# Adding a finished pair of rows to the residual with an accumulating DMA

## The chip, the cores and the metric

The kernel runs on one core of a Trainium2 chip. The metric is device microseconds of one execution; the median of three runs of the kernel before is 1159.39 us (1158.99 to 1159.63).

A core has engines that run beside each other, each with its own queue of instructions in a fixed order: TensorE (PE in the profile, matrix products; PEld are its weight loads), VectorE (DVE, element-wise work), ScalarE (ACT, element-wise functions and copies), GpSimd (POOL, element-wise work, and it issues transfers) and SyncE (SP, which here only issues transfers). Transfers (DMAs) are carried out by DMA engines. An instruction that needs another engine's result waits on a semaphore, and everything behind it in the same queue waits with it.

## The reference

Two transformer layers over 512 tokens of width 1024, in float32: a hybrid attention layer, a neighbourhood attention layer, and after each a squared-ReLU MLP whose result is added to the residual h. Cut to what matters:

```python
def sq_relu_mlp(h, w_up, w_down):
    u = jax.nn.relu(h @ w_up)
    return (u * u) @ w_down

for layer in range(DEPTH):                  # DEPTH = 2, D_MODEL = 1024, D_FF = 4096
    hn = rmsnorm(h, norm_mix[layer])
    h = h + attention(layer, hn)
    h = h + sq_relu_mlp(rmsnorm(h, norm_ffn[layer]), ffn_w_up[layer], ffn_w_down[layer])
return rmsnorm(h, final_norm)
```

## The kernel before

The residual lies transposed in SBUF as `hT`, 128 partitions x 8 blocks x 512 tokens; a block is 128 of the 1024 features. Every float32 operand of a product is split into a high and a low part, and a product is three matmuls (high x high, high x low, low x high).

The second product of each MLP (`u * u` times `w_down`) is cut in parts over the 4096 inner features (`mlp`, from line 1476):

- first an ordinary product over 6 inner blocks, written into `hT` by `ev` (L1505), one block at a time;
- then `product8`, over 10 inner blocks, also added by `ev`;
- then the seven-block product: `u7.run(ids[m], evac)` in the loop `for m in range(4)` (L1539 to L1546). It multiplies 2x2 blocks with seven products in place of eight. Each m makes two blocks (a pair of rows of blocks) of the result, over 14 inner blocks in layer 0 (7 chunks of weights) and 12 in layer 1 (6 chunks);
- last, an ordinary product over the remaining 2 (layer 0) or 4 (layer 1) inner blocks. In layer 0 it adds to `hT` with `ev` again (L1505). In layer 1 `last_mlp` does it with the tokens on the partitions: `turn` (L1919) transposes `hT` on TensorE, the first four blocks while the products of m = 2 and m = 3 run (`beside`, L1976), the last four in `down` after m = 3 (L1950).

A chunk of weights of the seven-block product (`seven_chunk`, L319) goes through four engines. SyncE issues its load of 256 KB (L324) into a slot of the shared pool (`Slot`, names `a` in the profile) if one is to be had, else into one of four `raw` buffers. GpSimd makes the four sums from it in three instructions (L326 to L328). ScalarE makes the high parts, `whi` (L332), VectorE the low parts, `wlo` (L333). TensorE uses the chunk in 21 matmuls (L418 to L420). A chunk is asked for five chunks ahead of its use (`LOAD`) and split two ahead (`AHEAD`). A later ordinary chunk is loaded at L211 or L214 and split at L233 and L223.

When the chunks of an m are done, `Seven.run` (L406) puts the pair together from the four PSUM banks in a slot `w_` of its own: one copy of ScalarE (L426) and four adds of VectorE (L427 to L430). Then `evac` (L1541) adds `w_` to the two blocks of `hT` (L1543), and the slot is given back (L432). Slots are given out first in, first out, so the slot of a finished pair soon takes a later chunk's weights, a later pair or a part of the next layer's input.

Nobody writes out the order of the instructions here: the framework's scheduler places each engine's instructions by its own estimate of when they can run, but for those marked to be kept in program order. After layer 0 the next layer's input is split by ScalarE and VectorE (L579, L580), its squares are summed (L587, L589), and TensorE reduces them (L594).

The chunks used in the loop over m are, in order of use, 7 for each m in layer 0 and 6 in layer 1. In layer 0 the slot of the first pair takes the last chunk of m = 1, that of the second pair the first chunk of m = 3; in layer 1 the slot of the first pair takes the first chunk of m = 2.

Of the kernel before, what the change touches and what calls it, by code (L numbers as in the profile page):

```python
# [12 lines left out]
ALU = mybir.AluOpType  # L13
# [22 lines left out]
def encoder_kernel(ctx: ExitStack, tc: tile.TileContext, ins, out, dbg=None):  # L36
    nc = tc.nc
    PE, ACT, DVE, POOL, SP = nc.tensor, nc.scalar, nc.vector, nc.gpsimd, nc.sync
# [299 lines left out]
    class Seven:  # L338
# [29 lines left out]
        def split(self, kp, held=lambda z: z):  # L368

            for b in range(7):  # L370
                i = self.number(kp, b) // 2
                if i not in self.slots:
                    self.slots[i] = Slot()
            raw, t = self.raw.pop(kp)
            own = isinstance(t, Slot)
            r, t_ = (s_.rearrange("p (b n) -> p b n", n=256) for s_ in (raw.t, t.t if own else t))

            T4 = t_[:, 2:3] if own else r[:, 3:4]
            src = lambda b, n: (r[:, 1 + b : 1 + b + n] if b < 3 else t_[:, b - 3 : b - 3 + n] if b < 5
                                else r[:, 0:1] if b == 5 else T4)  # L380
            b = 0
            while b < 7:
                q = self.number(kp, b)
                n = 2 if b == 3 or (b < 2 and q % 2 == 0) or (b == 5 and not own) else 1
                d = self.slots[q // 2].t.rearrange("p (q z n) -> p q z n", q=2, z=2)[:, q % 2 : q % 2 + n]
                s_ = r[:, 0:4:3] if b == 5 and n == 2 else src(b, n)
                ACT.activation(d[:, :, 0], s_, AF.Copy)
                held(DVE.tensor_tensor(d[:, :, 1], s_, f32(d[:, :, 0]), op=ALU.subtract))
                b += n
                yield  # L390
                if b == 3 and not own:
                    held(DVE.tensor_tensor(r[:, 3], r[:, 3], r[:, 0], op=ALU.subtract))
                    yield
            raw.free()
            if own:
                t.free()
# [94 lines left out]
    def product8(w, first, U, evac, eng=None):  # L491


        nk = len(U)
        ids = [plan([(0, D, rows(w, k, 1))], 1, D, None, eng) for k in first]

        def run():
            banks = group(4) + group(4)

            def one(k, j):  # L500

                wh, wl = (z[:, 0, P * j : P * j + P] for z in weights(ids[k], AHEAD - (k == 1 or k == nk - 1 and j < 7)))
                x = U[k].pair()
                mm3(banks[j], wh, wl, x[:, 0, :], x[:, 1, :], k == 0, k == nk - 1)


            for js in (range(4), range(4, 8)):
                for k in (0, 1):
                    for j in js:
                        one(k, j)  # L510
                        yield MM3
            U[0].free()
            U[1].free()
            for k in range(2, nk - 2):
                for j in range(8):
                    one(k, j)
                    yield MM3
                U[k].free()
            for j in range(8):
                for k in (nk - 2, nk - 1):  # L520
                    one(k, j)
                    yield MM3

                if j < 5:
                    evac(j, banks[j])
            for j in range(5, 8):
                tc.keep_in_program_order(evac(j, banks[j]))
            U[nk - 2].free()
            U[nk - 1].free()

        return run()
# [4 lines left out]
    def tiles(c0, n):  # L536
        return [(c0 + o, min(P, n - o)) for o in range(0, n, P)]
# [903 lines left out]
    def bias_rows():  # L1441
        R, Fi, Fe = Slot(F32), Slot(F32), Slot(F32)
        rpb = ins["od_rpb"][0]
        for qr in range(8):
            SP.dma_start(R.t[16 * qr : 16 * qr + 16, 0:248],
                           rpb.rearrange("h a b -> h (a b)")[:, (7 - qr) * 31 : (7 - qr) * 31 + 248])
            yield
        POOL.memset(Fi.t[:, 0:376], NEG)
        POOL.memset(Fe.t[:, 256:512], NEG)
        rv = R.t[:, 0:248].rearrange("p (k d) -> p d k", d=31)  # L1450
        POOL.tensor_copy(Fi.t[:, 0:376].rearrange("p (j k) -> p j k", k=8)[:, 15:31, :], rv[:, 7:23, :])
        POOL.tensor_copy(Fe.t[:, 0:248].rearrange("p (j k) -> p j k", k=8), rv)
        for _ in range(6):
            yield
        bxv = bx.rearrange("h t (c r) k -> t c r h k", r=8)
        for c in range(16):
            SP.dma_start(bxv[0, c].rearrange("r h k -> r h k"), Fi.t[:, (15 - c) * 8 : (15 - c) * 8 + 256])
            yield

            v, off = (1, (7 - c) * 8) if c < 8 else (0, (23 - c) * 8)  # L1460
            SP.dma_start(bxv[1, c][:, :, 128 * v : 128 * v + 128], Fe.t[:, off : off + 128])
            yield
            SP.dma_start(bxv[1, c][:, :, 128 - 128 * v : 256 - 128 * v], Fe.t[:, 256:384])
            yield
        for s_ in (R, Fi, Fe):
            s_.free()
        yield

    def convert(u7, R):
        held = tc.keep_in_program_order  # L1470
        for kp, raw in enumerate(R):
            yield from u7.sums(kp, raw, DVE, held)
            yield
            yield from u7.split(kp, held)

    def mlp(l, last=None):

        stage, ahead, later = first_product(l)
        reserve[0] = 3
        w = ins["ffn_w_down"][l]
        up4, gens4 = [], []

        def plain_last(k0, V):
            left = list(V)
            gens4.extend(product(w, k0, up4, tiles(512 * c, 512), lambda j, b, c=c: ev(4 * c + j, b), nk=2 * len(V))
                         for c in range(2))

            def beside(m, i):
                if m == 0 and i % 8 == 4 and left:
                    w_ = left.pop(0)
                    for z in range(2):
                        U4.append(Slot())
                        up4.append(U4[-1].pair())
                        split(w_.t[:, S * z : S * z + S], up4[-1])
                    w_.free()

            return beside  # L1500

        U4 = []

        def ev(m, b):
            return DVE.tensor_tensor(hT[:, m, :], hT[:, m, :], b, op=ALU.add)  # L1505

        U, _, _, (at_u, _), _ = stage(SIZES[l][0])
        up = [s_.pair() for s_ in U]
        gens = [product(w, at_u, up, tiles(512 * c, 512), lambda j, b, c=c: ev(4 * c + j, b)) for c in range(2)]
        ahead()  # L1510
        for c, gen in enumerate(gens):
            for i, _ in enumerate(gen):
                later(c, i)
        for s_ in U:
            s_.free()
        U, R, V, (at_u, at_r), late = stage(*SIZES[l][1:])
        first = [k + z for k in at_u for z in range(2)]
        gen = product8(w, first, U, ev)
        u7 = Seven(2 * len(R))
        ids = [u7.plan(w, 256 * m, at_r) for m in range(4)]  # L1520
        k0 = 32 - 2 * len(V)
        beside = (last or plain_last)(k0, V)
        bias = iter(()) if last else bias_rows()
        reserve[0] = NSLOT
        work, at = convert(u7, R), 0
        for i, _ in enumerate(gen):
            if i in (1, 4, 6):
                next(late, None)
            next(bias, None)

            at += 9 * len(R) + 2
            while at > 0:
                next(work, None)
                at -= 8 * len(U) - 2
        for x in (work, bias):
            for _ in x:
                pass
        reserve[0] = 1
        for m in range(4):  # L1539

            def evac(w_):  # L1541
                h2 = hT[:, 2 * m : 2 * m + 2, :]
                DVE.tensor_tensor(h2, h2, w_.t.rearrange("p (z n) -> p z n", z=2), op=ALU.add)  # L1543

            for i, _ in enumerate(u7.run(ids[m], evac)):
                beside(m, i)  # L1546
        u7.free()
        for gen in gens4:
            for _ in gen:
                pass  # L1550
        for s_ in U4:
            s_.free()
# [487 lines left out]
```

## Time and profile before

| What | us |
|---|---|
| median of the runs | 1159.39 |
| profiled execution, span from its first to its last instruction | 1157.2 |
| median of the runs less this span (start and end) | 2.2 |
| busy: TensorE | 1146.8 |
| busy: VectorE | 903.0 |
| busy: ScalarE | 652.1 |
| busy: GpSimd | 577.5 |

The profile is of one execution, which has no time of its own but its span; the runs that were timed lie within 0.64 us of each other. A row of the timeline gives the start in us, the duration in us, the engine, the line of the kernel, the operation, and out<-in with shapes; a number in square brackets is how long the engine sat idle before, and what ended that. Rows of grouped instructions give count, shortest, median and longest time in ns. A matmul is pipelined, so its start tells more than its end. SPq and POOLq are the queues of SyncE and GpSimd.

### The profile page before, as it was taken

What the parts mean: (1) busy time and instruction counts of PE and PEld (TensorE: products, weight loads), DVE (VectorE), ACT (ScalarE), POOL (GpSimd) and SP (SyncE); (2) the same over time, 40 slices, a digit from 0 to 9 for tenths busy, and PEclk for the clock granted to TensorE, in tenths of its full rate; (3) what the DMA queues carried; (4) which work ended last, traced back from release to release, by engine and by line L of the source; (5) the groups of instructions that cost most, each with busy time, mean ns of one, the idle gap of its engine ahead of it and who ended that gap; (6) DMA issues with size and microseconds to landing.
All of it is one profiled execution on the core that took longest, in us unless ns stands there. A gap on an engine that the chain in (4) does not pass through costs nothing.

```text
span 1157.2 us, 20288 instructions
## 1 busy us (share of the span) xinstructions
PE 1146.8 (99%) x7276; PEld 1021.1 (88%) x7276; DVE 903.0 (78%) x1542; ACT 652.1 (56%) x1115; POOL 577.5 (50%) x708
## 2 busy tenths in 40 slices
PE   9999999999999999999999999999999999999997
PEld 7787888888899999899988998988889999988996
DVE  7887988878978887877685666668987788778675
ACT  6676876755346667433454556555553666743345
POOL 4366252216798882379402232231379889316930
PEclk9999999999999999999999999999999999999999
DMA  8322415122432326523436664443333233432332
GB/s 241 100 74 70 101 51 142 55 67 98 126 93 74 92 83 202 185 92 117 125 98 164 150 174 128 117 109 117 100 120 108 79 89 92 136 102 80 98 106 73
DMA packets 112148, 128.05 MB, mean 111 GB/s; under 512 B 9411, under 2 KB 94576, under 8 KB 112048
## 3 DMA queue, kind: packets, MB, share of 16 engines
q1 hardware_dynamic: 109424, 120.09, 35.4%
q0 software_dynamic: 2304, 6.31, 2.3%
q8 instruction: 57, 0.93, 0.4%
q14 instruction: 43, 0.35, 0.1%
q10 hardware_dynamic: 320, 0.36, 0.1%
HBM read 104.32 MB, written 6.29 MB: 96 GB/s over the span
## 4 chain that ended last, share of the span: by engine, by line
PE 96%; DVE 2%; DMA 1%; issue 1%; ACT 0%; POOL 0%; DVEq 0%; POOLq 0%
PE mm L573 9%; PE mm L575 9%; PE mm L574 9%; PE mm L418 4%; PE mm L420 4%; PE mm L419 4%; PE s L1097 3%; PE t L418 3%; PE t L420 3%; PE t L419 3%; PE o L1085 3%; PE s L573 3%; PE s L574 3%; PE s L575 3%; PE s L418 2%; PE s L420 2%
## 5 line engine op out<-in xcount | busy, mean ns | idle before, releaser
L573 PE MATMUL mm<-a,whi 128*128 128x512 f32 x440 | 178.6, 407 | 0.2
L332 ACT ACTIVATE whi<-a 128x896 fp32r<-128x896 f32 x105 | 99.7, 951 | 132.5 <-POOL a L328 39.2
L574 PE MATMUL mm<-a,whi 128*128 128x512 f32 x440 | 173.5, 394 | 0.0
L575 PE MATMUL mm<-a,wlo 128*128 128x512 f32 x440 | 173.5, 395 | 0.0
L333 DVE TENSOR_TENSOR wlo<-a,whi 128x896 fp32r<-128x896 f32 x105 | 133.1, 1272 | 49.2 <-ACT whi L332 46.1
L223 DVE TENSOR_TENSOR wlo<-raw,whi 128x1024 fp32r<-128x1024 f32 (+4 forms) x113 | 131.1, 1164 | 39.0 <-ACT whi L233 38.4
L233 ACT ACTIVATE whi<-raw 128x1024 fp32r<-128x1024 f32 (+3 forms) x116 | 109.1, 942 | 68.4 <-PE s L574 24.0
L418 PE MATMUL mm<-a,whi 128*128 128x256 f32 x410 | 115.1, 281 | 0.0
L420 PE MATMUL mm<-a,wlo 128*128 128x256 f32 x410 | 114.7, 280 | 0.0
L419 PE MATMUL mm<-a,whi 128*128 128x256 f32 x410 | 114.7, 280 | 0.0
L328 POOL TENSOR_TENSOR a<-a 128x128 f32<-128x128 f32 x105 | 102.9, 980 | 8.2
L326 POOL TENSOR_TENSOR a<-a 128x128 f32<-128x128 f32 x105 | 75.8, 722 | 57.3 <-DMA a<-in_ffn_w_up_dram 37.1
L575 PEld LDWEIGHTS mm<-a,wlo 128*128 128x128 f32 x440 | 82.5, 188 | 18.9
L573 PEld LDWEIGHTS mm<-a,whi 128*128 128x128 f32 x440 | 82.7, 188 | 17.6 <-issue 0.6
L574 PEld LDWEIGHTS mm<-a,whi 128*128 128x128 f32 x440 | 82.9, 188 | 15.3 <-DVE a L930 0.2
L327 POOL TENSOR_TENSOR a<-a 128x256 f32<-128x256 f32 x105 | 90.6, 863 | 8.2
L333 DVE TENSOR_TENSOR wlo<-raw,whi 128x896 fp32r<-128x896 f32 x51 | 62.4, 1226 | 35.4 <-ACT whi L332 35.4
L1683 POOL TENSOR_SCALAR p<-p,ti 128x256 f32<-128x256 f32 x64 | 35.6, 567 | 104.7 <-DVE ti L1682 91.5
L1105 POOL TENSOR_SCALAR p<-p,ti 128x512 f32<-128x512 f32 x64 | 45.0, 705 | 85.7 <-DVE ti L1104 63.6
L418 PE MATMUL t<-a,whi 128*128 128x256 f32 x296 | 83.1, 281 | 0.0
L419 PE MATMUL t<-a,whi 128*128 128x256 f32 x296 | 82.8, 280 | 0.0
L420 PE MATMUL t<-a,wlo 128*128 128x256 f32 x296 | 82.8, 280 | 0.0
(427 smaller groups left out, 3492.9 us busy)
## 6 DMA issues: line engine op xcount, KB each, us to landing
a<-in_ffn_w_up_dram SPq DMA_DIRECT2D x78, 256.0 KB
raw<-in_ffn_w_down_dram SPq DMA_DIRECT2D x38, 512.0 KB
raw<-in_od_w_qkv_dram SPq DMA_DIRECT2D x64, 128.0 KB
a<-in_ffn_w_down_dram SPq DMA_DIRECT2D x27, 256.0 KB
raw<-in_ffn_w_up_dram SPq DMA_DIRECT2D x26, 256.0 KB
raw<-in_ffn_w_down_dram SPq DMA_DIRECT2D x25, 256.0 KB
raw<-in_ffn_w_up_dram SPq DMA_DIRECT2D x12, 512.0 KB
a<-a SPq DMA_DIRECT2D x18, 256.0 KB
```

The costliest lines, as they stand in the source:

```text
L223: z = lambda: (eng or DVE).tensor_tensor(to, src, f32(high), op=ALU.subtract)
L233: ACT.activation(hi[:, 0:m], raw[:, 0:m], AF.Copy)
L327: POOL.tensor_tensor(r[:, 4:6], r[:, 2:3].to_broadcast([P, 2, P]), r[:, 0:7:6], op=ALU.add)
L328: POOL.tensor_tensor(r[:, 7], r[:, 3], r[:, 5], op=ALU.subtract)
L332: ACT.activation(hi[:, 0:896], raw[:, 128:1024], AF.Copy)
L333: DVE.tensor_tensor(lo[:, 0:896], raw[:, 128:1024], f32(hi[:, 0:896]), op=ALU.subtract)
L418: PE.matmul(o, wh, x[:, 0], start=kp == 0 and n in (0, 1, 3, 5), stop=False, skip_group_check=True)
L419: PE.matmul(o, wh, x[:, 1], start=False, stop=False, skip_group_check=True)
L420: PE.matmul(o, wl, x[:, 0], start=False, stop=kp == self.np - 1, skip_group_check=True)
L573: PE.matmul(o, wh, xh, start=first, stop=False)
L574: PE.matmul(o, wh, xl, start=False, stop=False)
L575: PE.matmul(o, wl, xh, start=False, stop=last)
```

## The change

The add of L1543 is no longer an instruction of VectorE. GpSimd's queue issues a DMA that reads the pair `w_` (128 x 1024 float32, 512 KB) and adds it to the two blocks of `hT` in place. It is done eight times, four in each layer.

```diff
             def evac(w_):
                 h2 = hT[:, 2 * m : 2 * m + 2, :]
-                DVE.tensor_tensor(h2, h2, w_.t.rearrange("p (z n) -> p z n", z=2), op=ALU.add)
+                POOL.dma_start(h2, w_.t.rearrange("p (z n) -> p z n", z=2), accum_op=ALU.add)
```

What the scheduler makes of it, by the order of instructions in both programs: VectorE's queue loses eight instructions, GpSimd's gains eight issues. In layer 0 the DMA of m = 0 stands behind the sums of four chunks that are loaded into `raw` and `a` buffers and ahead of the sums of the chunk that takes slot 6190; that of m = 1 stands behind the sums of raw 6471; those of m = 2 and m = 3 stand behind all sums of the layer. In layer 1 the DMA of m = 0 stands behind the sums of the chunks in slots 12365 and 12406, that of m = 1 behind those of slot 12597, the other two behind all sums. The loads into the slots of the first pairs (6160, 6411 and 12436) now wait for the DMA in SyncE's queue, and each is put one place later among the loads and the sums. The transposes of L1919 that read a pair wait for its DMA; the first of them in layer 1 is put in two halves around three matmuls. In the next layer's input of layer 0, the split of one block (its slot is that of m = 3's pair) waits for that pair's DMA, and the reduction of the squares on TensorE (L594) stands some five matmuls earlier.

## The prediction

> **What bounds the kernel now.** I read the page's engine line, then the chain of waits, then line L1543 by itself.
>
> ```profile
> span 1157.2 us, 20288 instructions
> PE 1146.8 (99%) x7276; PEld 1021.1 (88%) x7276; DVE 903.0 (78%) x1542; ACT 652.1 (56%) x1115; POOL 577.5 (50%) x708
> PE 96%; DVE 2%; DMA 1%; issue 1%; ACT 0%; POOL 0%; DVEq 0%; POOLq 0%
> L1543 DVE TENSOR_TENSOR hT<-hT,a x8: 1218/1389/1556, 526.3 to 1128.9; 128x1024 f32<-128x1024 f32 x8
>   PEld mm L1919: 0.2, 1
> ```
>
> TensorE is busy for 1146.8 of 1157.2 us, so whatever VectorE is relieved of can hardly be gained; what counts is whether TensorE is made to wait. The eight adds cost VectorE some 8 x 1.39 = 11.1 us, and only one instruction ever waited for one, 0.2 us. Then I looked at the stretch that follows layer 0's first add, at ScalarE's waits around layer 1's first add, and at the chain where VectorE is on it.
>
> ```profile
> 522.50:540.00 17.50, 17.50 (x151) 17.50 (x150) 12.85 (x14) 6.94 (x9) 16.47 (x20) 1.00 0.34 106
> 586.72 1.40 DVE a L580 x3
> ACT whi L332 <- POOL a L328: 11.7, 5, 3.3
> ```
>
> The columns of the first row are time, TensorE, weight loads, VectorE, ScalarE, GpSimd, each with its instructions, then clock, DMA share and GB/s. GpSimd, 50% busy over the span, is 94% busy (16.47/17.50) here: it makes the sums of the next weight chunks, and ScalarE waits for them (third row, from 1079 to 1101 us, 11.7 us in five waits). The new DMA is put into this queue.
>
> **The change part by part.** Removed: eight VectorE adds, 11.1 us, beside TensorE work. The one place where VectorE sets the end is 586 to 598 us (second row above: there the chain of waits runs through it), and layer 0's last add, one of the short ones (1.22 us), lies ahead of it; at most 1.2 us is to be had there.
>
> Added: eight issues on GpSimd and eight landings that replace the end of the add. Their price:
>
> ```profile
> L1591 POOL DMA_DIRECT2D a<-a x16: 512/525/640, 610.6 to 755.0; - x16
> DMA to landing us min/median/max: 2.8/3.7/4.0
> a<-a POOLq DMA_DIRECT2D x16, 256.0 KB, 3.7
> a<-in_ev_a_q_norm_dram POOLq DMA_DIRECT2D x2, 0.2 KB, 3.3
> q0 software_dynamic: 2304, 6.31, 2.3%
> ```
>
> An issue holds GpSimd for 0.53 us; 8 x 0.53 = 4.2 us. No accumulating DMA and none of 512 KB from this queue is in the trace, so the landing L is bounded. Below: 3.3 us for 0.2 KB and 3.7 for 256 KB give 4.1 for 512 KB, if adding costs nothing. Above: the queue's 6.31 MB took 2.3% of the span, 26.6 us of all 16 engines, so 512 KB take 2.2 us; fetching the destination as well makes it 4.4, and 3.3 + 4.4 = 7.7. I take the middle, L = 6.0. The Trainium skill, "DMA: Bandwidth & Descriptors", section "Anatomy of one DMA — SWDGE (gpsimd) path", fits 2.0 us + bytes/436e3, an estimate of 3.2 us here; the 3.7 us for half the bytes says it is too short for this kernel, and by it the sum below would be about 6 us instead of 20.
>
> Three things now wait for a landing: the load that takes over the buffer of the finished pair (in SyncE's queue, with all loads behind it), the transposes of hT on TensorE, and the layer's last pair.
>
> *Layer 0, first pair.*
>
> ```profile
> 525.59 0.69 DVE L430 TENSOR_TENSOR a<-a,o 128x512 f32<-128x512 f32 x1
> 526.32 1.56 DVE L1543 TENSOR_TENSOR hT<-hT,a 128x1024 f32<-128x1024 f32 x1
> 526.87 1.33 POOL L328 TENSOR_TENSOR raw<-raw 128x128 f32<-128x128 f32 x1
> 527.90 0.37 SPq L324 DMA_DIRECT2D a<-in_ffn_w_down_dram  x1
> 532.35 0.46 POOL L326 TENSOR_TENSOR a<-a 128x128 f32<-128x128 f32 x1
> 534.12 0.46 POOL L326 TENSOR_TENSOR a<-a 128x128 f32<-128x128 f32 x1
> 535.19 2.43 DVE L333 TENSOR_TENSOR wlo<-a,whi 128x896 fp32r<-128x896 f32 x2 [3.11 <-ACT whi L332]
> 537.59 0.28 PE L420 MATMUL mm<-a,wlo 128*128 128x256 f32 x1
> ```
>
> Before, the add ends at 527.88 and the load into its buffer is issued at 527.90. That chunk's low parts are ready at 536.4 and used at 537.59: 1.2 us of slack. In the changed program's order the DMA stands behind the sums that end at 528.2, so it lands at 528.2 + 6 = 534.2 and frees the load only then. A load's own price:
>
> ```profile
> 1101.37 1.64 SPq L324 DMA_DIRECT2D a<-in_ffn_w_down_dram  x2
> 1104.09 0.47 POOL L326 TENSOR_TENSOR a<-a 128x128 f32<-128x128 f32 x1 [0.34 <-DMA a<-in_ffn_w_down_dram]
> 1087.44 0.95 ACT L332 ACTIVATE whi<-a 128x896 fp32r<-128x896 f32 x1 [2.40 <-POOL a L328]
> ```
>
> Load 2.8 us (1101.37 to 1104.09, and its issue), sums 1.9 at their fastest (532.35 to the next chunk's at 534.12, VectorE idle), high part 1.0, low part 1.2: 534.3 + 6.9 = 541.2. TensorE loses 541.2 - 537.6 = **3.6 us**.
>
> *Layer 0, second pair.* GpSimd's sums ahead of this DMA run on from 539.0 for the 11.9 us that the same four chunks took before (536.63 to 548.52), less some contention: issue at 550, landing 556, load, sums and splits to 563.
>
> ```profile
> 536.63 1.31 POOL L326 TENSOR_TENSOR raw<-raw 128x128 f32<-128x128 f32 x1
> 548.06 0.46 POOL L328 TENSOR_TENSOR raw<-raw 128x128 f32<-128x128 f32 x1
> 554.78 1.17 DVE L333 TENSOR_TENSOR wlo<-a,whi 128x896 fp32r<-128x896 f32 x1 [2.70 <-PE o L419]
> 557.41 0.28 PE L420 MATMUL mm<-a,wlo 128*128 128x256 f32 x1
> ```
>
> TensorE, already 3.6 late, wants it at 557.41 + 3.6 = 561.0: **2.0 us**.
>
> *Layer 0, last pair.* Nothing is ahead of this DMA. Landing at 578.7 + 6 = 584.7, while the next layer's third split (its buffer is the pair's) would run at about 583.
>
> ```profile
> 577.99 0.68 DVE L430 TENSOR_TENSOR a<-a,s 128x512 f32<-128x512 f32 x1
> 586.63 3.40 DVE L580 SCALAR_TENSOR_TENSOR a<-hT,gT,a 128x512 fp32r<-128x512 f32 x5
> ```
>
> The splits and adds behind it in VectorE's queue end at 590.6 instead of 590.03: **0.6 us**, the relief of 1.2 us already in it. Bounds -1.2 to 3.
>
> *Layer 1, first pair.*
>
> ```profile
> 1081.45 0.69 DVE L430 TENSOR_TENSOR a<-a,o 128x512 f32<-128x512 f32 x1
> 1086.94 0.46 POOL L328 TENSOR_TENSOR a<-a 128x128 f32<-128x128 f32 x1
> 1092.71 2.44 DVE L333 TENSOR_TENSOR wlo<-a,whi 128x896 fp32r<-128x896 f32 x2 [3.12 <-ACT whi L332]
> 1093.93 0.38 PE L420 MATMUL s<-a,wlo 128*128 128x256 f32 x1
> ```
>
> The pair is finished at 1082.1, but the DMA's place is behind two more chunks that GpSimd ends at 1087.4 (1086.8 without the add beside them). Landing 1092.8, the 6.9 us above: 1099.8. Here there is no slack: the low parts were ready at 1093.95, the matmul that needs them began at 1093.93 and took 0.38 instead of 0.28. **5.9 us.**
>
> *Layer 1, second pair.* Behind the late load stand the next loads, and the DMA's place is behind the sums of a chunk whose load waits until the low parts of the chunk after the late one are made (1100.9 instead of 1095.15):
>
> ```profile
> 1095.22 0.37 SPq L324 DMA_DIRECT2D a<-in_ffn_w_down_dram  x1
> 1098.86 1.22 DVE L1543 TENSOR_TENSOR hT<-hT,a 128x1024 f32<-128x1024 f32 x1
> 1099.77 0.80 PE L1919 MATMUL mm<-cst,hT 128*128 128x128 f32 x4
> 1103.29 0.46 POOL L328 TENSOR_TENSOR a<-a 128x128 f32<-128x128 f32 x1
> ```
>
> Load lands at 1103.8, sums to 1106.2 (before: 1103.75), DMA lands at 1112.2. The transposes that before met the end of the add (1100.08) now want these two rows at 1100.4 + 5.9 = 1106.3: another **5.9 us**. Without the first stall this one would be larger (1109.7 against 1100.4).
>
> *Layer 1, third and last pair.* The third has 15 us and hides behind the fourth product. The last:
>
> ```profile
> 1128.13 0.69 DVE L430 TENSOR_TENSOR a<-a,s 128x512 f32<-128x512 f32 x1
> 1132.33 0.60 PE L1919 MATMUL mm<-cst,hT 128*128 128x128 f32 x4
> ```
>
> Landing 1128.9 + 6 = 1134.9 against 1132.6: **2.3 us**. Layer 0's third pair is wanted 16 us later: nothing.
>
> Sum: 3.6 + 2.0 + 0.6 + 5.9 + 5.9 + 2.3 = 20.3, on a span of 1157.2: 1177.5. The median of the runs, 1159.39, is 2.2 above that span (start and end around it), so **1180 us**. With L = 4.1 the terms are 1.7, 0.1, -0.4, 4.0, 4.0, 0.4, sum 9.8: 1169. With 7.7: 5.3, 3.7, 2.3, 7.6, 7.6, 4.0, sum 30.5: 1190.
>
> **The rivals.** (a) The landing is much slower. GpSimd's own operations stretch from 0.46 to 1.33 us beside VectorE, loads share the engines (DMA share 0.34 in the stretches), and element-wise adding may run at a fraction of the copy. With L = 10 the terms are 7.6, 6.0, 4.6, 9.9, 9.9, 6.3, together 44: 1204. Against it, the sixteen 256 KB DMAs landed in 2.8 to 4.0 us beside the same kind of work. The Trainium skill, "SBUF — State Buffer", section "Who interferes with whom", lets a two-input VectorE operation block only GpSimd's reads, so by it descriptors would not be held up; no run shows that yet.
>
> (b) Only the waits for hT cost, because the load's buffer can be had earlier than I read (the sums of other chunks cover it). Then 9.3 (1109.7 - 1100.4) + 2.3 + 0.6 = 12.2: 1172. Against it stands the zero slack at 1093.93.
>
> (c) Not slower: VectorE's relief at 586 to 598 us decides, -1.2 us: 1158. This needs all landings to come no later than the adds ended. At the second pair of layer 1 that is 1100.08, with GpSimd reaching the DMA at 1103.75 before it can even issue; it would need a queue that is 10 us ahead of where it was.
>
> (d) The change isn't what it says: the add stays on the way of TensorE only in the last pair, since GpSimd runs ahead: 1162. Against it is its 94%.
>
> **How the numbers follow.** My forecast has 0.62, (a) 0.18, (b) 0.13, (c) 0.03, (d) 0.04. The forecast's own bounds are 1169 to 1190; (b) lies in them, and part of (a) is taken in up to 1200, leaving (c), (d) and the rest of (a) out; a little below 1169 covers sums at their fastest. Range 1167 to 1200. Runs of this kernel agree within 0.06%, and about 0.2% (2.3 us) can be told from no change; faster 0.02, same 0.03, slower 0.95.
>
> **What would show it.** On GpSimd, eight issues of about 0.5 us with L near 6. On TensorE, idle time where there was none: ahead of the chunk matmuls near 537, 561, 1094 us, 4 to 6 us in the third, put down to VectorE's or ScalarE's splits, and ahead of the hT transposes, put down to the DMA, some 6 and 2 us. SyncE's loads waiting for the DMA twice, four to nine us later than before. VectorE's busy time down by 11. I am wrong in the mechanism if TensorE's waits are less than 5 us in all, or if the loads don't wait; wrong in the size if L is outside 4 to 8; and wrong in the order if the second pair of layer 1 is issued well before 1104.

## The result and the profile after

The changed kernel takes 1178.83 us in the median of four runs (1176.19 to 1182.13), the kernel before 1159.34 us (1158.99 to 1159.63) beside it: 1.017 times as long, 95% interval 1.0152 to 1.0189. The execution that was profiled is the quickest of the four, 1176.19 us with a span of 1174.4, so the trace can explain only the 17.2 us by which this span is longer than that of before (1157.2); the other runs lie up to 5.9 us higher.

From the page of the changed kernel: the span, the engines' busy time, the shares of the chain of waits, and GpSimd's transfer queue (packets, MB, share of 16 engines).

```profile
span 1174.4 us, 20304 instructions
...
PE 1153.0 (98%) x7276; PEld 1026.0 (87%) x7276; DVE 891.5 (76%) x1534; ACT 652.5 (56%) x1115; POOL 571.6 (49%) x716
...
PE 84%; POOL 5%; DMA 4%; DVE 4%; issue 2%; ACT 1%; POOLq 0%; DVEq 0%; ACTq 0%
...
q0 software_dynamic: 3456, 10.50, 4.2%
```

The changed kernel's line L1543 by itself: how long an issue holds GpSimd in ns (shortest, median, longest), who waited for it (us, times), and the time to landing in us, which the row counts from the start of the issue.

```profile
L1543 POOL DMA_DIRECT2D hT<-a x8: 854/873/966, 528.0 to 1145.2; - x8
...
  PE mm L1919: 4.4, 2
  ACT a L579: 0.9, 1
...
DMA to landing us min/median/max: 4.5/4.9/6.2
```

VectorE is rid of 11.5 us (903.0 to 891.5) and the span is 17.2 us longer. The chain, which was 96% TensorE, now runs 13% of its way through GpSimd, the DMA and VectorE: links that used to lie beside TensorE's work. An issue holds GpSimd for 0.87 us. TensorE is also busy 6.2 us longer with the same 7276 matmuls, which no wait explains.

Where TensorE waits, by the view of waits (us in total, times, longest) of two stretches, the first layer's:

```profile
PE mm L418 <- ACT whi L332: 1.5, 1, 1.5
PE t L594 <- DVE acc L589: 1.1, 1, 1.1
PE mm L420 <- DVE wlo L333: 0.9, 2, 0.7
```

and the second layer's:

```profile
PE mm L1919 <- DMA hT<-a: 4.4, 2, 3.2
PE s L418 <- ACT whi L332: 2.8, 1, 2.8
PE s L420 <- DVE wlo L333: 0.4, 1, 0.4
```

In the kernel before, one of these waits is there, in the first layer's stretch:

```profile
PE t L594 <- DVE acc L589: 0.2, 1, 0.2
```

The view of the changed kernel's waits for SyncE:

```profile
SPq L324 <- DMA hT<-a: 18.0, 3, 6.9
```

Three loads wait for the DMA, 18.0 us together; all three reach TensorE as late chunks, that of layer 0's second pair by only 0.25 us. The waits of TensorE add up to 1.5 + 1.1 + 0.9 + 4.4 + 2.8 + 0.4 = 11.1 us, and they stand at the places where the timeline of TensorE shows them (start, duration, and in brackets the idle time ahead and what ended it):

```profile
538.78 0.38 PE L418 MATMUL mm<-a,whi 128*128 128x256 f32 x1 [1.50 <-ACT whi L332]
...
539.96 0.39 PE L420 MATMUL mm<-a,wlo 128*128 128x256 f32 x1 [0.68 <-DVE wlo L333]
...
561.76 0.38 PE L420 MATMUL mm<-a,wlo 128*128 128x256 f32 x1 [0.25 <-DVE wlo L333]
...
602.43 1.05 PE L594 MATMUL t<-ones,acc 128*128 128x1 f32 x8 [1.11 <-DVE acc L589]
...
1101.74 0.58 PE L418 MATMUL s<-a,whi 128*128 128x256 f32 x1 [2.79 <-ACT whi L332]
...
1102.92 0.58 PE L420 MATMUL s<-a,wlo 128*128 128x256 f32 x1 [0.38 <-DVE wlo L333]
...
1114.92 0.69 PE L1919 MATMUL mm<-cst,hT 128*128 128x128 f32 x2 [3.22 <-DMA hT<-a]
...
1149.76 0.44 PE L1919 MATMUL mm<-cst,hT 128*128 128x128 f32 x2 [1.20 <-DMA hT<-a]
```

These are the six places of the prediction, in its order. The matmuls right behind the waits at 1101.74 and 1102.92 take 0.58 us in place of 0.28 to 0.38. The view of stretches shows why: time, length, TensorE's busy time with its matmuls, granted clock (1.00 is full speed), DMA share, GB/s.

```profile
540.50:541.00 0.50, 0.50 (x6) 1.00 0.03 6
541.00:544.50 3.50, 3.50 (x20) 0.53 0.45 143
...
1100.00:1101.00 1.00, 0.00 (x0) 1.00 0.06 18
1101.00:1107.50 6.50, 5.37 (x23) 0.50 0.13 44
...
1108.00:1111.00 3.00, 3.00 (x28) 1.00 0.64 210
1115.00:1118.00 3.00, 3.00 (x15) 0.50 0.02 8
1118.50:1121.00 2.50, 2.50 (x24) 1.00 0.00 0
```

In the kernel before, the first of these stretches of half clock looked like this:

```profile
541.00:544.50 3.50, 3.50 (x32) 1.00 0.43 140
```

At three of the waits the clock falls, TensorE works at half of it for some us, and its matmuls stand twice as far apart (15 in 3.00 us, against 28 in 3.00). With the edges of these stretches read in slices of 0.1 us, the lost time (busy time times the missing share of the clock) is 1.7 us in layer 0, 2.9 and 1.6 in layer 1, 6.2 together. Of the waits, 0.2 us at the reduction were there before; 10.9 and 6.2 make 17.1 us of the 17.2 between the spans. That is closer than the method is: in the ten versions below that have no matmuls of ones, the same two sums come within 1.6 us of the difference of the spans.

So the theory to test, **A**: TensorE is set back only where something waits for a landing, by a late chunk (its buffer is still being read) or by a transpose of hT, and it pays a second time where the clock falls behind the wait. Against it stand **B**, each accumulating DMA costs about alike by GpSimd's queue or by traffic; **C**, the chunks are late because GpSimd's queue is longer, whatever the buffers do; **D**, relieving VectorE is worth something that the waits cover up; and for the clock **E**, it falls for a reason other than TensorE's idleness. Each run below stands beside fresh runs of the kernel before (1159.22 to 1159.46 us). Line numbers behind an edit are shifted by a few.

### The profile page after: what moved, and what is told of

Same layout as the page of the kernel before. It is cut to its first block, busy times and chain, and to the rows that moved or that the text cites. A ratio compares the mean times of both kernels' runs of the same rounds, so it can differ in the third digit from the quotient of the medians.

```text
span 1174.4 us, 20304 instructions
## 1 busy us (share of the span) xinstructions
PE 1153.0 (98%) x7276; PEld 1026.0 (87%) x7276; DVE 891.5 (76%) x1534; ACT 652.5 (56%) x1115; POOL 571.6 (49%) x716
## 3 DMA queue, kind: packets, MB, share of 16 engines
q0 software_dynamic: 3456, 10.50, 4.2%
## 4 chain that ended last, share of the span: by engine, by line
PE 84%; POOL 5%; DMA 4%; DVE 4%; issue 2%; ACT 1%; POOLq 0%; DVEq 0%; ACTq 0%
PE mm L573 9%; PE mm L575 8%; PE mm L574 8%; PE mm L420 3%; PE mm L418 3%; PE mm L419 3%; PE s L1097 3%; PE o L1085 3%; PE s L573 2%; PE s L574 2%; PE s L575 2%; DMA hT<-a 2%; PE t L1072 2%; PE t L418 2%; PE t L420 2%; PE t L419 2%
## 5 line engine op out<-in xcount | busy, mean ns | idle before, releaser
L326 POOL TENSOR_TENSOR a<-a 128x128 f32<-128x128 f32 x105 | 70.2, 668 | 71.0 <-DMA a<-in_ffn_w_up_dram 52.8
L327 POOL TENSOR_TENSOR a<-a 128x256 f32<-128x256 f32 x105 | 95.8, 912 | 8.2
L328 POOL TENSOR_TENSOR a<-a 128x128 f32<-128x128 f32 x105 | 92.7, 883 | 8.2
```

What stands on the lines that cost most here:

```text
L327: POOL.tensor_tensor(r[:, 4:6], r[:, 2:3].to_broadcast([P, 2, P]), r[:, 0:7:6], op=ALU.add)
L328: POOL.tensor_tensor(r[:, 7], r[:, 3], r[:, 5], op=ALU.subtract)
```

## The experiments

### One layer at a time, and only the covered pairs

Three versions put some pairs back on VectorE. `evac` of the first; the second has `l == 1`, the third `m == 2`:

```diff
-                POOL.dma_start(h2, w_.t.rearrange("p (z n) -> p z n", z=2), accum_op=ALU.add)
+                if l == 0:
+                    POOL.dma_start(h2, w_.t.rearrange("p (z n) -> p z n", z=2), accum_op=ALU.add)
+                else:
+                    DVE.tensor_tensor(h2, h2, w_.t.rearrange("p (z n) -> p z n", z=2), op=ALU.add)
```

> The four pairs of layer 0 go by DMA, those of layer 1 by VectorE as before. Theory A (TensorE waits at a few places for a landing, and runs at half clock for some us behind the longer gaps): layer 0's share of the measured shift, stalls 2.6 + 0.4 + 0.9 and 1.5 of slow clock, 5.4 us, so 1159.3 + 5.4 = 1164.7 us (1164 to 1166). Rival B (each accumulating DMA costs about alike, by GpSimd's queue or by traffic): half of the 19.5 us, 1169 us.

> The four pairs of layer 1 go by DMA, those of layer 0 by VectorE. Theory A: stalls 3.8 + 3.3 + 1.4 and slow clock 2.2 + 1.4, 12.1 us: 1171.4 us (1170 to 1174). Rival B (each DMA costs alike): 1169 us, and the two layers' shares equal.

> Only the third pair of each layer goes by DMA (two DMAs in all), the others by VectorE. Theory A: both landings are covered by the fourth product, no wait, no gap, full clock: 1159.3 us, within 0.5 of before. Rival B: a quarter of 19.5 us, 1164 us. The landing and the issue should be as in the changed kernel, 4.5 to 6.2 us and 0.9 us.

Measured: layer 0 alone 1165.21 us (ratio 1.0052, 1.0037 to 1.0067), layer 1 alone 1172.05 us (1.011, 1.0095 to 1.0125), both third pairs 1158.91 us (0.9998, 0.9989 to 1.0008). Over before's 1159.22 that is 6.0, 12.8 and -0.3 us; 6.0 + 12.8 = 18.8 of the 19.5 us of all eight. The two DMAs of the third version landed in 4.6 and 6.2 us, no quicker than the others:

```profile
L1544 POOL DMA_DIRECT2D hT<-a x2: 929/941/953, 563.5 to 1113.6; - x2
...
DMA to landing us min/median/max: 4.6/5.4/6.2
```

They cost nothing, since nobody waits for them. B, which wanted 1164 here and equal layers, is out: what costs is the wait, not the DMA.

### The first and the second pair of layer 1 by themselves

The same edit with `l == 1 and m == 0`, and with `l == 1 and m == 1`.

> Only the first pair of layer 1 goes by DMA. Theory A: the load of the first chunk of m = 2 waits for the landing; TensorE stalls 3.8 us near 1095 us and runs one or two stretches at half clock behind it (1.7 each): 1159.4 + 5.5 to 7.2 = 1165 to 1166.6 us, and no wait for the transposes. If slot and transposes were not separate causes, the time would be 1160 or 1171.

> Only the second pair of layer 1 goes by DMA. By the prediction's step the stall is larger without the first one: GpSimd comes to this DMA at 1103.8 as before, issues 0.9 us and lands 4.9 us later at about 1109.5, the transposes want it at 1100.4: 9 us, and 1.7 to 3.4 of half clock, 1170 to 1172 us. Rival F (as with the held slots, GpSimd comes to it by 1100.5): 4.6 + 1.7, 1165.7 us.

Measured: 1164.07 us (1.0045, 1.0027 to 1.0063) and 1168.91 us (1.0081, 1.0065 to 1.0097), 4.8 and 9.7 us over before. Each came out a little under its forecast. From the view of waits of the first version:

```profile
PE s L418 <- ACT whi L332: 1.7, 1, 1.7
PE s L420 <- DVE wlo L333: 0.7, 1, 0.7
```

From the timelines of GpSimd and TensorE of the second:

```profile
1103.63 0.94 POOL L1544 DMA_DIRECT2D hT<-a  x1
...
1108.72 0.69 PE L1922 MATMUL mm<-cst,hT 128*128 128x128 f32 x2 [7.19 <-DMA hT<-a]
```

With the first pair alone only the late chunk is waited for; no transpose waits. Its 2.4 us of waits and one stretch at half clock (1.7 us lost) make 4.1 of the 4.3 us by which the span is longer. So buffer and transposes are two causes, each with a price of its own. With the second pair alone the transposes wait 7.19 us in place of 3.22. The DMA comes 6 us earlier than in the changed kernel (1103.63 against 1109.57), but the transposes come earlier still, since no late chunk holds TensorE up ahead of them. The two causes overlap: 4.8 + 9.7 = 14.5 by themselves, and the whole of layer 1, last pair included, costs 12.8.

### Taking the waits away

In the first version the slots of the first two pairs are not given back until the loop has ended, so that no load can wait for them. In the second the first four transposes are all done during m = 3. The third has both edits, and in the fourth the last pair goes by VectorE as well (six pairs by DMA).

```diff
+        kept = []
         reserve[0] = 1
         for m in range(4):
...
+                if m < 2:
+                    kept.append(w_)
+                    return True
...
+        for s_ in kept:
+            s_.free()
```

```diff
-                if m > 1 and i in (16, 22):
-                    turn(2 * (m - 2) + (i == 22), 0)
+                if m == 3 and i in (4, 10, 16, 22):
+                    turn((4, 10, 16, 22).index(i), 0)
```

> All eight pairs by DMA, but the slots of the first and second pair of each layer are given back only behind the last pair, so that no load of the loop waits for a DMA; chunks that took those slots use others or raw buffers. Theory A: the stalls of layer 0's first and second pair and of layer 1's first go with their slow clock (4.1 + 0.4 + 6.0 us); the transposes of hT then come earlier and wait longer, some 8 us and 1.5 to 2 of slow clock, and the last pairs keep 0.9 and 1.4: together 12 to 13 us, 1171 to 1173 us, with no wait of SyncE for the DMA in the loop. Rival C (the late chunks come from GpSimd's queue being longer, not from the slot): TensorE still waits near 538 and 1099 for low or high parts, time near 1178.8 us.

> The changed kernel, but the first four transposes of hT in layer 1 all come during m = 3 (at its steps 4, 10, 16, 22) in place of m = 2 and m = 3; slots as in the changed kernel. Theory A: the wait of 3.2 us and the half clock behind it (4.7 us together) go, the slot waits stay (6.0 us at layer 1's first pair): 1178.8 - 4.7 = 1174.1 us. Rival C (GpSimd's queue or the load's lateness sets TensorE back whatever the transposes do): no change, 1178.8 us, the lost time turning up at later chunks of m = 3.

> Both edits: the first two pairs' slots kept to the end of the loop and the transposes put into m = 3, all eight pairs by DMA. Theory A: no wait of TensorE on a landing is left but those of the last pairs, 0.9 in layer 0 and 1.4 in layer 1 at most: 1161 to 1162 us, full clock throughout layer 1's products. Rival B (each DMA costs something of its own): 1167 us as with the slots alone, or more than 1163 us.

> As hold_and_late, and the last pair of each layer by VectorE as before, so six of eight pairs by DMA. Theory A: every landing is covered, nothing waits: 1159.3 us as before, within 1 us (1158.3 to 1160.3); VectorE's busy time some 8 us less than before brings nothing, since TensorE is busy all the time. Rival D (relieving VectorE is worth something once no wait hides it): 1158 us or less.

| version | median us | ratio to before, 95% |
|---|---|---|
| slots held | 1167.05 | 1.0068 (1.0053 to 1.0083) |
| transposes late | 1170.08 | 1.0091 (1.0075 to 1.0106) |
| both | 1161.20 | 1.0016 (1.0007 to 1.0026) |
| both, last pair by VectorE | 1159.43 | 0.9999 (0.9989 to 1.0008) |

With the slots held, TensorE has no wait for a late chunk in either layer, and SyncE none for the DMA. C is out, for GpSimd has the same eight issues and is busy no less (577.6 us against 571.6). The forecast of 1171 to 1173 was too high because of the transposes. I expected them to wait some 8 us, and they waited 3.4:

```profile
1100.46 0.88 POOL L1544 DMA_DIRECT2D hT<-a  x1
...
1105.58 0.69 PE L1925 MATMUL mm<-cst,hT 128*128 128x128 f32 x2 [3.44 <-DMA hT<-a]
```

The edit also changes which chunks go to slots and which to raw buffers, and with them GpSimd's queue: it comes to this DMA at 1100.46, not at 1103.63 as in the version with the second pair alone.

With the transposes late, the wait of 3.22 us is gone, and nothing takes its place. The time fell by 8.7 us and not by 4.7. The spans of the two profiled executions are 6.4 us apart (1174.4 and 1168.0). Between them the waits in the two layers' stretches fall by 3.4 us (11.1 to 7.7), and the time lost at half clock by 4.5 and not by 1.5: here one stretch at half clock (from 1103.1 us, 1.7 us lost) stands against three in the changed kernel, one of these a double. Against these 7.9 us stand 1.4 us more of idle time in the first 300 us, where no pair is added. The other 2.3 us between the medians no profile shows. As the waits of the chunks were nearly as before (1.1 and 0.7, 2.8 and 0.7 us), that already says that such a stretch doesn't follow each wait.

With both, the waits left are those of the last pairs (view of waits of "both"):

```profile
PE t L594 <- DVE acc L589: 0.7, 1, 0.7
PE mm L1925 <- DMA hT<-a: 1.2, 1, 1.2
```

Without them the time is before's. The engines' busy time on the page of "both, last pair by VectorE":

```profile
PE 1146.3 (99%) x7276; PEld 1020.5 (88%) x7276; DVE 892.8 (77%) x1536; ACT 653.1 (56%) x1115; POOL 575.1 (50%) x714
```

The step from 1161.20 to 1159.43 is the price of the last pairs, 1.8 us. In the last version VectorE is 10.2 us less busy than before (892.8 against 903.0), six DMAs run, and the time is before's within 0.1%. D is out: the relief from these six adds is worth nothing that can be measured where TensorE is busy 99% of the span.

### The half clock

Does the clock fall because TensorE idles? In the first version twelve matmuls of ones (24 instructions in the profile) stand ahead of the second half of the transpose that waits 3.22 us; the wait for the landing stays.

```diff
             for q in range(4):
+                if (i, c, q) == (0, 0, 2):
+                    for _ in range(12):
+                        PE.matmul(b[:, 256:384], ones, ones, start=True, stop=True)
                 PE.transpose(b[:, q * P : (q + 1) * P], hT[:, 4 * c + q, i * P : (i + 1) * P], ident)
```

> The changed kernel with twelve matmuls of ones put right ahead of the second half of the first transpose in layer 1, the place where TensorE waits 3.2 us; they write a part of the bank that the transposes then overwrite. The wait for the landing stays. Theory A' (the half clock follows from TensorE's idleness): the granted clock stays at 1.00 in the 4 us behind that transpose (0.50 for 3 us in the changed kernel), and the matmuls there start 0.12 us apart; 1.4 us less, too little to be told in the time of one run. Rival E (the low clock comes with the landing DMA or with other load of the chip at that time): 0.50 again for some 3 us. The gap near 1101 us isn't filled and must show 0.50 by both.

From its timeline of TensorE:

```profile
1114.18 2.84 PE L1921 MATMUL mm<-ones 128*128 128x128 f32 x24
...
1117.40 0.44 PE L1922 MATMUL mm<-cst,hT 128*128 128x128 f32 x2 [0.38 <-DMA hT<-a]
```

and from its view of stretches:

```profile
1117.70:1121.00 3.30, 3.30 (x31) 1.00 0.00 1
...
606.50:609.50 3.00, 3.00 (x8) 0.50 0.16 49
```

The DMA lands, the transposes wait for it as before, but TensorE is idle for 0.38 us in place of 3.22, and the clock stays at 1.00 where it was 0.50. This is what A forecast, and E had the clock fall again. It is one execution; what all profiles together say of it stands in the last section. At the unfilled gap the clock fell as before, for 6.8 us from 1104.5 us. The one time was 1177.59 us, which says nothing of 1.7 us.

The last row is a stretch at half clock behind the wait of the reduction (L594), here 1.2 us long; in the changed kernel, with 1.1 us at this place, there was none (602.5 to 610 us at 1.00). The versions with layer 0 alone and with the slots held had one there too. A second version then filled three gaps: eight matmuls of ones ahead of the late chunk of layer 0, twelve ahead of that of layer 1, and the twelve above. `idle_work(n, b)` (L157) runs n such matmuls into the bank b.

```diff
-        def run(self, ids, evac):
+        def run(self, ids, evac, gap=()):
...
                 hi, lo = weights(ids[kp])
...
+                if gap and kp == gap[0]:
+                    idle_work(gap[1], gap[2]())
                 for n, ((a, b), (i, z)) in enumerate(zip(SEVEN, dst)):
...
-            for i, _ in enumerate(u7.run(ids[m], evac)):
+            gap = {(0, 1): (6, 8, ob), (1, 2): (0, 12, mmb)}.get((l, m))
+            for i, _ in enumerate(u7.run(ids[m], evac, gap)):
```

> The changed kernel with matmuls of ones in three gaps of TensorE: eight ahead of the late chunk in layer 0 (last chunk of m = 1), twelve ahead of the late chunk in layer 1 (first chunk of m = 2), twelve ahead of the second half of the first transpose; the waits themselves stay. Theory A' (half clock follows from idleness, in stretches of about 3.3 us that cost 1.7 us each, one or two behind a gap and none behind a gap that is filled): no half clock near 541, 1101 and 1115 us; the time falls to before plus the stalls, 1159.4 + 12.2, with at most one stretch behind the unfilled gap of the reduction near 602 us: 1171.6 to 1173.3 us, and the runs spread over less than 2 us (the changed kernel's over 6). Rival E (the low clock has another cause, or the matmuls of ones cost what they fill): 1176 us or more.

Measured: 1175.84 us (1173.3 to 1177.1; ratio 1.0146, 1.0128 to 1.0164), over its forecast of 1171.6 to 1173.3 and just under the 1176 of E; the runs spread over 3.8 us, where less than 2 was expected. The filling in layer 1 went wrong, as the timelines of TensorE (two rows) and VectorE show:

```profile
1101.54 2.94 PE L157 MATMUL mm<-ones 128*128 128x128 f32 x24 [3.03 <-ACT a L428]
...
1104.24 0.36 PE L420 MATMUL s<-a,whi 128*128 128x256 f32 x1
...
1099.87 2.40 DVE L333 TENSOR_TENSOR wlo<-a,whi 128x896 fp32r<-128x896 f32 x2 [6.49 <-ACT whi L332]
```

The matmuls of ones themselves waited 3.03 us for a PSUM bank that ScalarE had still to read, and then ran from 1101.54 to 1104.24, although the late chunk's low part, the first of the two in the last row, had been done at 1101.1 (half of 2.40 behind 1099.87). So the chunk's first matmul came 3.1 us after that instead of at once, and with that the forecast would have been 1174.7 to 1176.4 (an estimate). The time doesn't test what the version was made for. In the profiled execution (1173.3 us) no stretch at half clock followed, not even the unfilled 3.03 us. That a gap of this length is always enough, this version denies; how a gap must lie is worked out in the last section.

### What adding costs

> The changed kernel with a plain copy in place of the accumulating one: the residual is left out (each pair overwrites hT). Tells what of the landing is size and what is adding. Theory G (adding costs a second pass over part of the way): landing 4.1 us (3.3 + 2 x 0.4), issue as with the add; six stalls shorter by 0.8 us, 1174 us. Rival H (adding is free, the size alone sets it): landing 4.9 us, 1178.8 us.

```diff
-                POOL.dma_start(h2, w_.t.rearrange("p (z n) -> p z n", z=2), accum_op=ALU.add)
+                POOL.dma_start(h2, w_.t.rearrange("p (z n) -> p z n", z=2))
```

Measured: 1168.47 us (1.0076, 1.0057 to 1.0095). Its rows for the same eight transfers:

```profile
L1543 POOL DMA_DIRECT2D hT<-a x8: 527/570/648, 527.9 to 1138.6; - x8
...
DMA to landing us min/median/max: 2.9/3.7/5.9
```

and its page's row of the queue:

```profile
q0 software_dynamic: 3456, 10.50, 3.2%
```

Neither G nor H is met, and G is nearer: the copy of 512 KB lands in 3.7 us, as the 256 KB copies before did, so doubling the bytes costs nothing here, and adding costs 1.2 us of landing and 0.3 us of issue. The queue's share for the same 10.50 MB falls from 4.2% to 3.2%. Less the 26.6 us of before, eight adds take 22.7 us of all 16 engines (4.2% of 1174.4, less 26.6), eight copies 10.7 (3.2% of 1167.1, less 26.6): an add occupies them about twice as long. (The shares are rounded to 0.1%, 1.2 us, so this is an estimate.) The span of the profiled execution is 7.3 us shorter than with the add (1167.1 against 1174.4), the median 10.4. TensorE's waits for the splits, the reduction's sum and the transposes add up to 5.7 us in place of 11.1, and the time lost at half clock, worked out as above, to 3.3 in place of 6.2.

## Why the prediction was right, step by step

Forecast 1180 us, measured 1178.83; the mechanism was right in its places, but the total hides two errors of opposite sign, so that its coming within 1.2 us is in part luck. Each term beside the profiled execution (waits from the timeline, slow clock from the stretches):

| place | forecast | wait | slow clock | together |
|---|---|---|---|---|
| layer 0, first pair | 3.6 | 2.2 | 1.7 | 3.9 |
| layer 0, second pair | 2.0 | 0.2 | 0 | 0.2 |
| layer 0, last pair | 0.6 | 0.9 | 0 | 0.9 |
| layer 1, first pair | 5.9 | 3.2 | 2.9 | 6.1 |
| layer 1, second pair | 5.9 | 3.2 | 1.6 | 4.8 |
| layer 1, last pair | 2.3 | 1.2 | 0 | 1.2 |
| sum | 20.3 | 10.9 | 6.2 | 17.1 |

- **The price of a landing was too high.** "I take the middle, L = 6.0" met 4.9 us. The lower bound supposed that doubling the bytes adds 0.4 us; the copy shows that it added nothing, so the bound of 4.1 was itself an over-estimate, 3.7 us. What adds is the adding, 1.2 us. The upper bound gave an add 4.4 us of all 16 engines; by the estimate above it took 2.8 (22.7 for eight). Six waits by 1.1 us take 6.6 off the sum of 20.3, to 13.7; the other 2.8 to 10.9 are small pieces of the chains (in layer 1 the first DMA was issued 4.2 us after its pair was finished, forecast 4.7; the sums at their fastest take 1.8 us by the rows, not 1.9). The rule weighed there, 2.0 us + bytes/436e3 (the Trainium skill, "DMA: Bandwidth & Descriptors", section "Anatomy of one DMA — SWDGE (gpsimd) path"), gives 3.2 us: 0.5 under the copy, 1.7 under the accumulating DMA.
- **The issue was priced too low,** 0.53 us after copies of half as many partitions; it is 0.87. As the landing is counted from the issue's start, this is in the 4.9, and GpSimd's queue alone pays the rest, which showed nowhere.
- **The clock was not in the sum at all.** 6.2 of the 17.2 us are matmuls at half clock, and they nearly make up for the landing. The idle time forecast near 1094 us, "4 to 6 us in the third", was 3.2. That the first term of layer 1 was nearly met (6.1 for 5.9) is chance: 3.2 of wait and 2.9 of clock.
- **Both kinds of wait are real.** Rival (b), that only the transposes cost, falls with the first pair of layer 1 alone (4.8 us, no transpose waiting) and with the held slots; rival (d) with 10.9 us of waits at six places, of which the last pairs' are 2.1. Rival (a) needed 10 us of landing; the longest in the changed kernel was 6.2. Rival (c) forecast 1158 us and is out by the time. Its 1.2 us of relief lie behind layer 0's last add; in every version that takes that add from VectorE the landing takes its place, so what the relief is worth by itself is not shown.
- **"Without the first stall this one would be larger"** was right: 7.19 us against 3.22 with the second pair alone (3.44 with the slots held, where GpSimd came to the DMA 3 us sooner).
- **The three signs:** the loads waited for the DMA three times (forecast two); GpSimd's second issue in layer 1 came at 1109.57, which less the 5.0 us that layer 0 had lost by then (3.9 + 0.2 + 0.9) is 1104.6, so not well before 1104 (forecast 1106.2); VectorE's busy time fell by 11.5 (forecast 11).

Open: the four runs of the changed kernel spread over 5.9 us, the four of before beside them over 0.6 (19 later ones over 2.6). Only the quickest was profiled. Longer lost time at half clock would do it, and so would longer landings (4.5 to 6.2 us in one execution). The clock alone does not: the mean granted clock is 0.992, 0.992, 0.993 and 0.990 for 1176.19, 1177.92, 1179.73 and 1182.13 us, so the second longest run has the highest. No run settles the rest.

## What to carry to other kernels

An instruction taken off an engine that doesn't set the end gains nothing, and the operation that takes its place is priced by who waits for its end: list the buffers it holds and the readers it feeds, and look for the slack of each. Where TensorE is busy all the time, a wait of two or three us can cost another 1.6 to 2.9 us, because the clock may fall at it. Pairs with 15 us to the next reader went by DMA for nothing, and with the slots held and the readers moved away so did six of the eight.

## What the runs showed of the hardware

Around the changed pairs a stretch at half clock was 3.4 or 6.8 us long wherever there was one, and two in one execution began 13.65 us apart (1101.01 and 1114.66), four times 3.413. TensorE's waits of 1.1 to 3.2 us were followed by one in some executions and not in others at the same place: the reduction's wait of 1.1 to 1.2 us in three versions but not in the changed kernel and two more, a wait of 3.03 us not at all.

The Trainium skill, "TensorE: Matmul & The Clock Gate", section "Part 1: The HAM clock gate", has a window of 3413 ns that runs by itself, and half clock after an idle one. The length and the chance in it agree with these runs. That a whole window must be idle does not: 2.2 us of idle time in two pieces (1.50 and 0.68) were enough here.

What decides is how much idle time falls into one window. In each of the 14 profiles of this case all edges of the granted clock lie whole multiples of 3.413 us apart, so the windows can be laid out (541.22, 1101.01 and 1114.66 us in the changed kernel are 164 and 4 of them apart) and TensorE's idle time in each added up from its rows. The reduction's eight one-column matmuls are counted as idle here. Of the windows at full clock up to 1140 us, some 4,600, all 14 with 1.80 us or more of idle time were followed by half clock, of the five with 1.65 to 1.76 us two were, and of the others none: by these numbers the limit is near half a window, 1.7 us.

The waits above then fall into place. The 1.50 and 0.68 us had 1.65 us in one window; the 3.03 us without a stretch lay in two windows, 1.27 and 1.76 us; the reduction's three windows with a stretch held 1.9 to 2.1 us, those without at most 1.65. The gap that was filled would have held 2.6 us in one window (1114.76 to 1118.17), and 0.38 were left. So no stretch of half clock came without idle time, and the remaining theory, E, has no case among the 16 stretches. That one-column matmuls count as idle is inferred from the three stretches at the reduction; no run varied it.
